# Operands of block products at alternating byte offsets, by the parity of their inner index

## Chip, cores and metric

The kernel runs on one core of one Trainium2 chip. The metric is the device time of one execution in microseconds (us). The kernel before the change takes 1253.34 us, the median of three runs (1251.72 to 1253.52).

## What is computed

A decoder trunk of two layers on 512 tokens with 1024 channels, in float32. Layer 0 mixes tokens by attention in three head groups with different dilation, layer 1 by causal pooling; a SwiGLU feed-forward network (FFN) with 2816 hidden channels follows each.

```
for i in range(DEPTH):                       # 2 layers
    if i % 2 == 0: x = x + dilated_attention_mixer(rmsnorm(x, attn_norm), w_qkv, w_attn_out)
    else:          x = x + pooling_mixer(rmsnorm(x, pool_norm), w_pool_in, w_pool_group, pool_scale)
    x = x + swiglu_ffn(rmsnorm(x, ffn_norm[i]), w_ffn_gate_up[i], w_ffn_down[i])
return rmsnorm(x, final_norm)

def swiglu_ffn(h, w_gate_up, w_down):
    gu = h @ w_gate_up
    gate, up = gu[..., :D_FF], gu[..., D_FF:]
    return (jax.nn.silu(gate) * up) @ w_down
```

## The kernel before, in words

Channels lie on the 128 partitions and tokens along them, so that a tile of 128 channels is 128x512, 2048 bytes in each partition. Every float32 matrix product is made of float32r matmuls: each operand is cut into a high part (a copy on ACT, line 96) and a low part (a subtraction on DVE, line 97), and one product of 128x128 weights with an operand takes three matmuls, high by high, high by low and low by high. Below, such three are called a **triple**. The weights are the stationary side and the operand, made from activations, is the moving side; only the attention values (lines 553 to 555) have it the other way round.

There are two kinds of products. Plain products (`Product.add`, lines 272, 273 and 275) stream 512 columns a matmul: the first q and k rows, w_out, the first five gate/up pairs of each FFN, the last part of w_down, and the pooling mixer. Block products (Strassen's seven products in place of eight) stream 256 columns: `seven` and `values12` for q, k and v, with `mult` inside (lines 391 to 393), and `chain` for the FFN's gate/up pairs and most of w_down. A product sums over an inner index k: 8 tiles in a plain product, 4 half tiles in a block product, 3 in the blocks of the FFN's second and third group. So a plain product is 24 matmuls and a block product 12 or 9, one triple for each k, all triples one behind the other on TensorE.

Operands live in **slots**, tiles of 4096 bytes in a partition: the high part in the first half, the low part in the second. Twelve slots (`FIXED`) lie in the pool `cpool`, sixteen (`SLOTS`) in the pool `fpool` that opens after the attention. `slot` takes the slot that has been free longest from one queue, and `give` puts it back. For the attention's block products some operands (`tx`) also lie in the X tiles, which are free at that time. The names of operands are h, t and tx (attention), h (plain FFN products), tb, tt and tn (gate/up pairs), hx, hy, hz and hu (w_down's blocks), a (the last hidden tiles), oh (attention's output), n and y (pooling).

Where a tile begins in its partition follows from the sizes of the tiles before it. In the built program, the X tiles and the twelve `FIXED` slots begin 128 bytes behind a multiple of 256; so do all weight tiles (whi, wlo, halfhi, halflo, in `wpool`); the sixteen slots of `fpool` begin at multiples of 256. The steps inside a tile (2048 bytes from high to low part, 1024 between halves, 512 between weight blocks) are multiples of 256. An operand and the weights are called **in phase** below when both begin alike modulo 256, and **out of phase** when they differ by 128.

The instructions of each engine run in its own order, which a scheduler fixes when the program is built, from the dependencies of the tiles: a tile that is written into a slot waits until the slot's last readers are through, and the scheduler may put it further back in an engine's order for that. Weights are loaded by SP's queue and by POOL's (the summed halves, line 158), cut by `pump` while products run, and freed when their product is through.

Of the kernel before, what the change touches and what calls it, by code (L numbers as in the profile page):

```python
# [8 lines left out]
F32 = mybir.dt.float32  # L9
F32R = mybir.dt.float32r  # L10
# [5 lines left out]
P = 128  # L16
S = 512
D = 1024
KC = D // P
# [17 lines left out]
K2 = KC // 2  # L37
# [5 lines left out]
FIXED = 12  # L43
SLOTS = 16
# [7 lines left out]
def trunk(ctx: ExitStack, tc: tile.TileContext, xT, norms, w_first, w_qk, w_qkp, w_v0, w_v0p, w_v12, w_out, w_pair, w_down, w_down0, w_down1, w_down2, w_pin, w_pgrp,  # L52
          consts, ident_in, invcnt_in, outT):
    nc = tc.nc
    cpool = ctx.enter_context(tc.tile_pool(name="cpool", bufs=1))
# [4 lines left out]
    def x_tile(k, name="x", dtype=F32):  # L60
        return cpool.tile([P, S], dtype, tag=f"x{k}", name=name)

    X = [x_tile(k) for k in range(KC)]
    nrm = cpool.tile([P, NORMS, KC], F32, name="nrm")
    ident = cpool.tile([P, P], F32, name="ident")
# [212 lines left out]
            return self  # L278


    free, pools = deque(range(FIXED)), {i: cpool for i in range(FIXED)}

    def slot(name, dtype=F32R):
        i = free.popleft()
        t = pools[i].tile([P, 2, S], dtype, tag=f"slot{i}", name=name, bufs=1)
        return i, t

    held = {}

    def give(key):  # L290
        free.append(held.pop(key))

    operand = {}

# [8 lines left out]
    def square(layer, k, engine=None):  # L303
        if layer not in acc:
            acc[layer] = tmp.tile([P, S], F32, name="acc", bufs=1)
            nc.scalar.activation(acc[layer], X[k], AF.Square)
            return
        sq = scratches[-1]("sq")
        nc.scalar.activation(sq, X[k], AF.Square)
        (engine or nc.vector).tensor_add(acc[layer], acc[layer], sq)  # L310

    def scaled(layer, k, hi, lo, on_dve=False):

        g = nrm[:, layer, k:k + 1]
        if on_dve:
            nc.vector.tensor_scalar(hi, X[k], g, None, op0=OP.mult)
        else:
            nc.scalar.activation(hi, X[k], AF.Copy, scale=g)
        nc.vector.scalar_tensor_tensor(lo, X[k], g, hi.bitcast(F32), op0=OP.mult, op1=OP.subtract)
        operand[layer, k] = hi, lo  # L320

    def note(layer, k):

        if layer < 4:
            held[layer, k], t = slot("h")
            scaled(layer, k, t[:, 0], t[:, 1])
        square(layer, k)

# [192 lines left out]
    with tc.tile_pool(name="opool", bufs=1) as opool:  # L521
        early = opool.tile([P, HEADS, S], F32R, tag="o", name="early")
        with tc.tile_pool(name="apool", bufs=1) as apool:
# [240 lines left out]
            H, T, o = {}, {}, []  # L764

            def prepare(k):

                h, t = Held("raw"), Held("raw")
                normed(0, k, rows["row"], h.t, t.t)
                for i in range(2):  # L770
                    held["h", k + i * K2], b = slot("h")
                    H[k + i * K2] = b[:, 0], b[:, 1]
                    split(*H[k + i * K2], h.t[:, i * S:(i + 1) * S])
                T["11", k] = halves_of(*H[k])[0]
                T["21", k], T["22", k] = halves_of(*H[k + K2])
                for i, names in enumerate((("1", "2"), ("3", "4"))):
                    if k < 2:
                        held["t", k, i], b = slot("t")
                        b = b[:, 0], b[:, 1]
                    else:  # L780
                        c = k - 2 + 2 * i
                        b = x_tile(c, "tx", F32R), x_tile(c + K2, "tx", F32R)
                    split(*b, t.t[:, i * S:(i + 1) * S])
                    for name, v in zip(names, halves_of(*b)):
                        T[name, k] = v
                h.done()
                t.done()
# [131 lines left out]
            for m in range(KC):  # L919
                if lead:  # L920
                    f = lead.pop(0).add([last])
                else:
                    f = Product(HEADS, heads).add(range(HEADS))
# [5 lines left out]

    with tc.tile_pool(name="fpool", bufs=1) as fpool:  # L930
        fpool.tile([P, 32], F32, name="shift", bufs=1)
        for i in range(FIXED, FIXED + SLOTS):
            free.append(i)
            pools[i] = fpool

        def unfold(m, p):

# [9 lines left out]
        def ffn(layer, nxt, lead, row, wk):  # L947
# [3 lines left out]
            pieces, T, TH, hid, act = deque(), {}, [{} for g in GROUPS], {}, []  # L951
# [3 lines left out]

            def wide(key, name):

                held[key], t = slot(name, F32)
                return t.rearrange("p a c -> p (a c)")

            def raw_hidden(j):
# [7 lines left out]
            def hide(j, gt, up):  # L969

                if j >= FC - LAST:
                    nc.vector.tensor_mul(up, up, gt)
                    held["a", j], t = slot("a")
                    act.append((t[:, 0], t[:, 1]))
                    split(*act[-1], up)
                    return
                hid[j] = raw_hidden(j)
                nc.vector.tensor_mul(hid[j], up, gt)
                g, = [g for g, (a, b) in enumerate(GROUPS) if a <= j < b]
                pieces.extend(blocks_of(g, (j - GROUPS[g][0]) // 2, hid[j - 1], hid[j]) if j % 2 else  # L980
                              half_of(g, (j - GROUPS[g][0]) // 2, hid[j]))
# [8 lines left out]
            def half_of(g, i, a):  # L990
                t = TH[g]

                def corner():
                    held["hb", g, i, 0], t["x", i] = slot("hx")
                    t["t", i] = wk.tile([P, 2 * S], F32, name="t", bufs=1)
                    t["11", i] = cut(two(t["x", i], 0), a[:, lo])

                def first():
                    v = t["t", i][:, :H2]
                    nc.vector.tensor_sub(v, a[:, hi], a[:, lo])  # L1000
                    t["1", i] = cut(two(t["x", i], 1), v)

                return corner, first

            def blocks_of(g, i, a, b):
                t = TH[g]

                def row2():
                    held["hb", g, i, 1], y = slot("hy")
                    split(y[:, 0], y[:, 1], b)  # L1010
                    t["21", i], t["22", i] = two(y, 0), two(y, 1)

                def middle():
                    v = t["t", i]
                    nc.vector.tensor_sub(v[:, H2:S], v[:, :H2], b[:, hi])
                    nc.vector.tensor_sub(v[:, S:3 * H2], b[:, hi], a[:, hi])
                    held["hb", g, i, 2], z = slot("hz")
                    split(z[:, 0], z[:, 1], v[:, H2:3 * H2])
                    t["2", i], t["3", i] = two(z, 0), two(z, 1)

                def fourth():
                    v = t["t", i]
                    nc.vector.scalar_tensor_tensor(v[:, 3 * H2:], v[:, H2:S], -1.0, b[:, lo], op0=OP.mult, op1=OP.subtract)
                    if i % 2 == 0:
                        held["hb", g, i, 3], t["u"] = slot("hu")
                    t["4", i] = cut(two(t["u"], i % 2), v[:, 3 * H2:])
                    key = ("hr", (GROUPS[g][0] + 2 * i) // 2)
                    if key in held:
                        give(key)

                return row2, middle, fourth
# [14 lines left out]
            def prepare(k):  # L1046


                h, t = wide(("hp", k), "hp"), wide(("tp", k), "tp")
                normed(op, k, row, h, t, True)  # L1050
                hq, b22 = h.rearrange("p (a b c) -> p a b c", a=2, b=2), h[:, 3 * H2:]
                held["t", k, 0], b = slot("tb")
                split(b[:, 0].rearrange("p (a c) -> p a c", a=2), b[:, 1].rearrange("p (a c) -> p a c", a=2), hq[:, :, 0])
                T["11", k], T["21", k] = two(b, 0), two(b, 1)
                for i, names in enumerate((("1", "2"), ("3", "4"))):
                    held["t", k, 1 + i], b = slot("tt")
                    split(b[:, 0], b[:, 1], t[:, i * S:(i + 1) * S])
                    for a, name in enumerate(names):
                        T[name, k] = two(b, a)
                if k % 2 == 0:  # L1060
                    held["t", k, 3], T["n"] = slot("tn")
                T["22", k] = cut(two(T["n"], k % 2), b22)
                give(("hp", k))
                give(("tp", k))
# [108 lines left out]
        with tc.tile_pool(name="pooling", bufs=6) as wk:  # L1173
# [38 lines left out]
            def mix(g):  # L1212
                for c in range(2):
                    f = Product(2, lambda k: Y[g][k], w=wg[g // 2, g % 2]).add(range(2), pos=2 * c)
                    m = 2 * g + c
                    nc.vector.scalar_tensor_tensor(X[m], f.p, nrm[:, 5, m:m + 1], X[m],
                                                   op0=OP.mult, op1=OP.add)
                    held[3, m], t = slot("n")
                    scaled(3, m, t[:, 0], t[:, 1])
                    square(3, m, nc.gpsimd)  # L1220
                for c in range(2):
                    give(("y", g, c))
# [17 lines left out]
        with tc.tile_pool(name="work1", bufs=1) as wk:  # L1240
# [46 lines left out]
            f = end(7, 1)  # L1287
# [4 lines left out]
            t = wk.tile([P, 2 * S], F32, name="t", bufs=1)  # L1292
# [87 lines left out]
```

## Time and profile before

| what | value |
|---|---|
| time, three runs | 1253.34 us median, 1251.72 to 1253.52 |
| time of the profiled execution | 1251.78 us |
| its span, first to last instruction | 1250.0 us |
| TensorE (PE) busy | 1237.6 us, 99%, 9072 matmuls |
| VectorE (DVE) busy | 1013.6 us, 81% |
| ScalarE (ACT) busy | 679.7 us, 54% |
| GpSimd (POOL) busy | 154.9 us, 12% |
| granted TensorE clock, mean | 0.996 |
| DMA | 189.91 MB, 152 GB/s over the span |

A matmul's duration in the profile is longer than its share of TensorE's time, since matmuls overlap: a 256-column matmul is shown with 0.28 us, while the next starts about 0.12 us later. What a matmul costs is therefore read from starts: a stretch of time divided by the number of matmuls that start in it. A view of a stretch counts the two or three that are still running at its begin as well.

The attention's block products lie between about 90 and 440 us, w_out up to 505, the first FFN from 509 to 840, pooling to 907, the second FFN to the end.

### The profile page before, as it was taken

What the parts mean: (1) busy time and instruction counts of PE and PEld (TensorE: products, weight loads), DVE (VectorE), ACT (ScalarE), POOL (GpSimd) and SP (SyncE); (2) the same over time, 40 slices, a digit from 0 to 9 for tenths busy, and PEclk for the clock granted to TensorE, in tenths of its full rate; (3) what the DMA queues carried; (4) which work ended last, traced back from release to release, by engine and by line L of the source; (5) the groups of instructions that cost most, each with busy time, mean ns of one, the idle gap of its engine ahead of it and who ended that gap; (6) DMA issues with size and microseconds to landing.
All of it is one profiled execution on the core that took longest, in us unless ns stands there. A gap on an engine that the chain in (4) does not pass through costs nothing. (4 is left out here: it accounts for less than half of the span.)

```text
span 1250.0 us, 23243 instructions
## 1 busy us (share of the span) xinstructions
PE 1237.6 (99%) x9072; PEld 1174.0 (94%) x9072; DVE 1013.6 (81%) x1687; ACT 679.7 (54%) x1171; POOL 154.9 (12%) x147
## 2 busy tenths in 40 slices
PE   9999999999999999999999999999999999999997
PEld 7889999999999988889999999988789999999997
DVE  7987788878778846798777878798989877888876
ACT  6444554445455544466466557563446646656652
POOL 2011111112111010101111111000310111111100
PEclk9999999999999999999999999999999999999998
DMA  8336566655756434437776786653144777677742
GB/s 291 110 85 170 134 156 145 163 131 159 182 132 161 132 138 136 113 81 194 187 186 158 177 208 163 153 181 118 51 119 117 182 182 178 153 205 190 174 116 68
DMA packets 76719, 189.91 MB, mean 152 GB/s; under 512 B 7600, under 2 KB 15936, under 8 KB 76608
## 3 DMA queue, kind: packets, MB, share of 16 engines
q1 hardware_dynamic: 51696, 142.26, 35.7%
q0 software_dynamic: 24336, 45.63, 22.5%
q8 instruction: 71, 1.16, 0.4%
q10 hardware_dynamic: 576, 0.52, 0.1%
q14 instruction: 40, 0.33, 0.1%
HBM read 186.29 MB, written 2.10 MB: 151 GB/s over the span
## 5 line engine op out<-in xcount | busy, mean ns | idle before, releaser
L96 ACT ACTIVATE whi<-raw 128x1024 fp32r<-128x1024 f32 (+2 forms) x315 | 318.7, 1016 | 248.3 <-PE seed L392 76.1
L97 DVE TENSOR_TENSOR wlo<-raw,whi 128x1024 fp32r<-128x1024 f32 (+2 forms) x315 | 367.1, 1169 | 105.3 <-ACT whi L96 104.5
L158 POOL DMA_DIRECT2D raw<-w_pair x34 | 41.1, 1209 | 310.5 <-ACT whi L96 75.4
L391 PE MATMUL sum<-tt,whi 128*128 128x256 f32 x272 | 77.0, 283 | 1.5 <-ACT seed L477 0.8
L392 PE MATMUL sum<-tt,whi 128*128 128x256 f32 x272 | 76.7, 282 | 0.0
L393 PE MATMUL sum<-tt,wlo 128*128 128x256 f32 x272 | 76.5, 281 | 0.0
L96 ACT ACTIVATE halfhi<-rawhalf 128x512 fp32r<-128x512 f32 (+1 forms) x87 | 53.2, 612 | 19.8 <-PE sum L392 12.4
L173 DVE TENSOR_TENSOR raw<-raw 128x512 f32<-128x512 f32 (+1 forms) x87 | 57.6, 662 | 2.1 <-issue 2.0
L174 DVE TENSOR_TENSOR raw<-raw 128x512 f32<-128x512 f32 (+1 forms) x87 | 57.7, 663 | 0.2
L97 DVE TENSOR_TENSOR halflo<-rawhalf,halfhi 128x512 fp32r<-128x512 f32 (+1 forms) x87 | 57.6, 664 | 0.0
L158 POOL DMA_DIRECT2D raw<-w_down x24 | 28.9, 1206 | 215.2 <-DMA raw<-w_down 34.4
L391 PEld LDWEIGHTS sum<-tt,whi 128*128 128x128 f32 x272 | 51.4, 189 | 1.9 <-ACT seed L477 1.0
L477 ACT COPY seed<-sum 128x256 f32<-128x256 f32 x58 | 20.8, 359 | 57.7 <-PE sum L393 57.5
L392 PEld LDWEIGHTS sum<-tt,whi 128*128 128x128 f32 x272 | 51.3, 189 | 0.0
L393 PEld LDWEIGHTS sum<-tt,wlo 128*128 128x128 f32 x272 | 51.2, 188 | 0.0
L391 PE MATMUL sum<-hz,whi 128*128 128x256 f32 x160 | 45.4, 284 | 0.5 <-ACT seed L477 0.3
L392 PE MATMUL sum<-hz,whi 128*128 128x256 f32 x160 | 45.3, 283 | 0.0
L392 PE MATMUL seed<-hy,whi 128*128 128x256 f32 x160 | 45.3, 283 | 0.0
L393 PE MATMUL seed<-hy,wlo 128*128 128x256 f32 x160 | 45.2, 283 | 0.0
L393 PE MATMUL sum<-hz,wlo 128*128 128x256 f32 x160 | 45.2, 283 | 0.0
L391 PE MATMUL seed<-hy,whi 128*128 128x256 f32 x160 | 45.1, 282 | 0.0
L158 POOL DMA_DIRECT2D raw<-w_qkp x18 | 22.0, 1222 | 166.4 <-DMA raw<-w_qkp 102.1
(610 smaller groups left out, 4631.7 us busy)
## 6 DMA issues: line engine op xcount, KB each, us to landing
raw<-w_pair SPq DMA_DIRECT2D x78, 512.0 KB, 4.7
raw<-w_qkp SPq DMA_DIRECT2D x36, 512.0 KB, 4.6
raw<-w_pair POOLq DMA_DIRECT2D x34, 512.0 KB, 7.6
raw<-w_down SPq DMA_DIRECT2D x32, 384.0 KB, 3.9
raw<-w_v SPq DMA_DIRECT2D x18, 512.0 KB, 4.1
raw<-w_qkp POOLq DMA_DIRECT2D x18, 512.0 KB, 7.4
rawhalf<-w_pair SPq DMA_DIRECT2D x34, 256.0 KB, 4.5
raw<-w_down SPq DMA_DIRECT2D x16, 512.0 KB, 4.9
```

Of the source, the lines that this page charges most:

```text
L96: nc.scalar.activation(hi, v, AF.Copy)
L97: nc.vector.tensor_tensor(lo, v, hi.bitcast(F32), op=OP.subtract)
L158: nc.gpsimd.dma_start(b.rearrange("p (a c) -> p a c", a=2), self.src[:, None, 3 * q:].to_broadcast([P, 2, q]), accum_op=OP.add)
L173: nc.vector.tensor_add(a[:, :q], a[:, :q], b[:, :q])
L174: nc.vector.tensor_add(a[:, q:2 * q], a[:, q:2 * q], a[:, :q])
L391: nc.tensor.matmul(dst, w.t[0][:, c], th, start=k == 0 and not onto, stop=False, skip_group_check=onto)
L392: nc.tensor.matmul(dst, w.t[0][:, c], tl, start=False, stop=False, skip_group_check=onto)
L393: nc.tensor.matmul(dst, w.t[1][:, c], th, start=False, stop=k == n - 1, skip_group_check=onto)
L477: nc.scalar.copy(e, c)
```

## The change

Slots get a side: `spread_over` makes the first half of a pool's slots, then a tile of 128 bytes (`apart`), then the second half, so that one half begins at multiples of 256 bytes and the other 128 behind. `slot` takes a slot of the side that is asked for, and one of the other side when there is none; each side has its own queue of free slots. The X tiles are laid out anew: those of odd k first, a gap of 128 bytes, those of even k. In the built program the weights still begin 128 bytes behind a multiple of 256. Side 0 is at multiples of 256 (out of phase), side 1 is in phase.

The side is the parity of the inner index k for the operands of block products; for tn and hu, where one slot holds two inner indices, it is that of k // 2. Operands of plain products ask for side 1, except oh and y, which take the default 0, as the slots for raw values do.

```
+    for k in (*range(1, KC, 2), None, *range(0, KC, 2)):
+        if k is None:
+            cpool.tile([P, 32], F32, name="gap")
+        else:
+            x_tile(k)
...
-    free, pools = deque(range(FIXED)), {i: cpool for i in range(FIXED)}
-
-    def slot(name, dtype=F32R):
-        i = free.popleft()
+    pools = {}
+    free = [[], []]
+
+    def spread_over(pool, n):
+
+        for kind in range(2):
+            for i in range(len(pools), len(pools) + n // 2):
+                pools[i] = pool
+                side[i] = kind
+                free[kind].append(i)
+                pool.tile([P, 2, S], F32R, tag=f"slot{i}", name="new", bufs=1)
+            if kind == 0:
+                pool.tile([P, 32], F32, name="apart", bufs=1)
+
+    def slot(name, dtype=F32R, kind=0):
+        i = (free[kind] or free[1 - kind]).pop(0)
         t = pools[i].tile([P, 2, S], dtype, tag=f"slot{i}", name=name, bufs=1)
         return i, t
...
-        free.append(held.pop(key))
+        i = held.pop(key)
+        free[side[i]].append(i)
+
+    side = {}
+    spread_over(cpool, FIXED)
...
-            held[layer, k], t = slot("h")
+            held[layer, k], t = slot("h", kind=1)
...
-                    held["h", k + i * K2], b = slot("h")
+                    held["h", k + i * K2], b = slot("h", kind=k % 2)
...
-        for i in range(FIXED, FIXED + SLOTS):
-            free.append(i)
-            pools[i] = fpool
+        spread_over(fpool, SLOTS)
...
-                    held["hb", g, i, 0], t["x", i] = slot("hx")
+                    held["hb", g, i, 0], t["x", i] = slot("hx", kind=i % 2)
...
-                        held["hb", g, i, 3], t["u"] = slot("hu")
+                        held["hb", g, i, 3], t["u"] = slot("hu", kind=i // 2)
```

The other `slot` calls for t, tb, tt, tn, hy, hz, a and n change in the same way. No instruction is added or removed.

By the addresses in the two built programs, a triple of a block product in `mult` follows one of the other phase 570 times of 2099 before and 1799 times with the change; in the attention's `seven` never before and 587 times of 587 with it. Of the 1320 matmuls with 512 columns, 264 are out of phase before (168 of h, 60 of n, 36 of y) and 156 with the change (96 of oh, 60 of h).

The order of instructions is the same on SP and POOL, and on all engines in the attention. It changes in the FFN, since slots are handed out in another order. On ACT, at the end of the first FFN's second group (L469 and L477, with the change L490 and L498, copy a running sum within a w_down chain; hx are the first two operands of the third group), before:

```order
L1082 COPY up<-sum 128x256
L469 COPY seed<-sum 128x256
L96 ACTIVATE hx<-hid 128x256
L96 ACTIVATE hx<-t 128x256
L477 COPY seed<-sum 128x256
L96 ACTIVATE whi<-raw 128x768 x3
```

and with the change, three chains of w_down further on:

```order
L101 ACTIVATE whi<-raw 128x768
L101 ACTIVATE whi<-raw 128x1024 x2
L101 ACTIVATE halfhi<-rawhalf 128x512
L490 COPY seed<-sum 128x256
L101 ACTIVATE hx<-hid 128x256
L101 ACTIVATE hx<-t 128x256
L498 COPY seed<-sum 128x256
```

The two hx copies move from the first to the last of the group's four w_down chains, behind the read of the slot that they now take. On DVE the two subtractions that belong to them move along; with the change they stand here, ahead of a weight tile's low part:

```order
L102 TENSOR_TENSOR halflo<-rawhalf,halfhi 128x512
L1114 TENSOR_TENSOR x<-x,seed 128x256
L102 TENSOR_TENSOR hx<-hid,hx 128x256
L102 TENSOR_TENSOR hx<-t,hx 128x256
L102 TENSOR_TENSOR wlo<-raw,whi 128x1024
```

Both move in the same way in the second FFN. Near the begin of the first FFN, among its plain gate/up pairs, ACT's copy of one hy moves from before a Silu to behind the next two copies of tt, and a later hx copy moves forward past it; before the change the piece reads:

```order
L96 ACTIVATE hx<-hr 128x256
L96 ACTIVATE hy<-hr 128x512
L1043 ACTIVATE gt<-gt 128x512
L96 ACTIVATE tb<-hp 128x512
L96 ACTIVATE tn<-hp 128x256
L96 ACTIVATE whi<-raw 128x1024
L96 ACTIVATE tt<-tp 128x512 x2
```

and with the change:

```order
L101 ACTIVATE hx<-hr 128x256
L1062 ACTIVATE gt<-gt 128x512
L101 ACTIVATE tb<-hp 128x512
L101 ACTIVATE tn<-hp 128x256
L101 ACTIVATE whi<-raw 128x1024
L101 ACTIVATE tt<-tp 128x512 x2
L101 ACTIVATE hy<-hr 128x512
```

The hy copy is now the last of these. On PE, in each FFN one triple of a gate/up pair changes places with part of the w_down product beside it.

More of the change, by code (lines that the diff above doesn't have):

```diff
@@ L777, in prepare @@
                     if k < 2:
-                        held["t", k, i], b = slot("t")
+                        held["t", k, i], b = slot("t", kind=k % 2)
                         b = b[:, 0], b[:, 1]
@@ L956, in wide @@
             def wide(key, name):
-                held[key], t = slot(name, F32)
+                held[key], t = slot(name, F32, kind=0)
                 return t.rearrange("p a c -> p (a c)")
@@ L972, in hide @@
                     nc.vector.tensor_mul(up, up, gt)
-                    held["a", j], t = slot("a")
+                    held["a", j], t = slot("a", kind=1)
                     act.append((t[:, 0], t[:, 1]))
@@ L1008, in row2 @@
                 def row2():
-                    held["hb", g, i, 1], y = slot("hy")
+                    held["hb", g, i, 1], y = slot("hy", kind=i % 2)
                     split(y[:, 0], y[:, 1], b)
@@ L1016, in middle @@
                     nc.vector.tensor_sub(v[:, S:3 * H2], b[:, hi], a[:, hi])
-                    held["hb", g, i, 2], z = slot("hz")
+                    held["hb", g, i, 2], z = slot("hz", kind=i % 2)
                     split(z[:, 0], z[:, 1], v[:, H2:3 * H2])
@@ L1051, in prepare @@
                 hq, b22 = h.rearrange("p (a b c) -> p a b c", a=2, b=2), h[:, 3 * H2:]
-                held["t", k, 0], b = slot("tb")
+                held["t", k, 0], b = slot("tb", kind=k % 2)
                 split(b[:, 0].rearrange("p (a c) -> p a c", a=2), b[:, 1].rearrange("p (a c) -> p a c", a=2), hq[:, :, 0])
@@ L1055, in prepare @@
                 for i, names in enumerate((("1", "2"), ("3", "4"))):
-                    held["t", k, 1 + i], b = slot("tt")
+                    held["t", k, 1 + i], b = slot("tt", kind=k % 2)
                     split(b[:, 0], b[:, 1], t[:, i * S:(i + 1) * S])
@@ L1060, in prepare @@
                 if k % 2 == 0:
-                    held["t", k, 3], T["n"] = slot("tn")
+                    held["t", k, 3], T["n"] = slot("tn", kind=k // 2)
                 T["22", k] = cut(two(T["n"], k % 2), b22)
@@ L1217, in mix @@
                                                    op0=OP.mult, op1=OP.add)
-                    held[3, m], t = slot("n")
+                    held[3, m], t = slot("n", kind=1)
                     scaled(3, m, t[:, 0], t[:, 1])
```

## Prediction

> **What bounds the kernel now.** First the page: TensorE is the engine that is never free. Busy time alone could hide waiting, so the waits of TensorE come next.
>
> ```profile
> span 1250.0 us, 23243 instructions
> PE 1237.6 (99%) x9072; PEld 1174.0 (94%) x9072; DVE 1013.6 (81%) x1687; ACT 679.7 (54%) x1171; POOL 154.9 (12%) x147
> ...
> PEclk9999999999999999999999999999999999999998
> ```
>
> ```profile
> PE seed L812 <- DVE idle L809: 1.2, 1, 1.2
> PE sum L391 <- ACT seed L477: 1.1, 2, 0.8
> PE ps L350 <- POOL rcol L342: 1.1, 1, 1.1
> PE sum L391 <- ACT seed L469: 0.8, 2, 0.7
> ```
>
> The four longest groups of waits come to 4.2 us of 1250, and the granted clock is full throughout. So TensorE works through one stream, and what counts is the time from one matmul's start to the next. A change of addresses acts on that, or not at all; DVE and ACT matter only where they could make the stream wait.
>
> The view by stretches shows what a matmul takes. I chose stretches that begin and end at a start of a matmul, without a wait inside, and whose phases (from the addresses) are pure.
>
> ```profile
> core 0: us, PE busy (x), PEclk, DMA share, GB/s
> 158.47:171.31 12.84, 12.84 (x110) 1.00 0.52 121
> 509.31:550.61 41.30, 41.30 (x184) 1.00 0.50 123
> 566.54:570.81 4.27, 4.27 (x38) 1.00 0.25 68
> 560.00:720.00 160.00, 160.00 (x1340) 1.00 0.73 179
> 795.03:796.70 1.67, 1.67 (x17) 1.00 0.56 99
> 802.66:804.32 1.66, 1.66 (x17) 1.00 0.62 205
> 801.02:804.20 3.18, 3.18 (x30) 1.00 0.72 209
> 856.25:861.12 4.87, 4.87 (x22) 1.00 0.62 159
> ```
>
> The count includes matmuls still running at the begin (three in the rows with x110, x17 and x30, two with x38, x184 and x1340, one with x22); by starts:
>
> - 158.47: block products of the attention, all in phase: 12.84/107 = 120.0 ns a matmul of 256 columns.
> - 566.54: gate/up products on tt and tn, all out of phase: 4.27/36 = 118.6 ns.
> - 795.03 and 802.66: w_down's blocks, the phase changing at every triple, five triples of which the first and the last are in phase: 1.67/14 = 119.3 and 1.66/14 = 118.6 ns.
> - 801.02: the same blocks where the phase goes out, in, in, out, in, in, out, in, out: 3.18/27 = 117.8 ns, the lowest over that length in the trace.
> - 509.31: plain products of the first FFN, in phase: 41.30/182 = 226.9 ns a matmul of 512 columns.
> - 856.25: plain products on h, out of phase: 4.87/21 = 231.9 ns.
> - 560 to 720, the first FFN's block part with today's mixed phases: 160.00/1338 = 119.6 ns; 17 steps in it are longer than 130 ns, by 1.2 us together, mostly at a first half weight, and without these it is 118.7 ns.
>
> So phase shows in the trace, in opposite directions: plain products want equal phase (5.0 ns of 232), block products want anything but constant equal phase (1.4 ns of 120). These rows come from different stages, which I return to among the rivals.
>
> The Trainium skill, "SBUF — State Buffer" (Who interferes with whom), gives TensorE two independent read ports, for the moving operand and for the weights, and says that it never waits on anyone; by it no byte offset would change a matmul's time and the sum below would be zero. The 231.9 beside 226.9 ns at equal shapes speak against it.
>
> **The change part by part.**
>
> 1. Attention, `seven`: 588 triples, 1764 matmuls, all in phase today at 120.0 ns (the row at 158.47). With the change all alternate. The alternating rows give 119.3 and 118.6; I take 118.9, their middle. 1764 x 1.1 = **-1.9 us**. Bounds: -3.9 us at 117.8, -1.2 at 119.3, and 0 if offsets not seen so far behave like equal phase.
>
> 2. Attention, `values12`: 224 triples, 672 matmuls, in which the operand is the stationary side and the weights stream. Today all are in phase; which side is shifted has no row. Bounds: 0, and the same 1.1 ns as in 1, 0.7 us. I take half, **-0.4 us**; a loss as large isn't excluded, since plain products show that out of phase can cost.
>
> 3. FFN, `chain`: 1512 triples, 4536 matmuls. Here the phases are mixed already and 118.7 ns is what there is to beat. Changes between triples go from 570 of 1511 to 1212. Strict alternation (118.9) gives nothing; but where one slot holds two inner indices (tn, hu) the pattern is pairs, and in the groups of three inner indices the last triple of one product and the first of the next have the same phase, as in the row at 801.02. I take 118.5, between 118.7 and the best row, nearer to the former since most products have four inner indices: 4536 x 0.2 = **-0.9 us**. Bounds: 117.8 gives -4.1 us, 119.3 gives +2.7, and 120.0 gives +5.9.
>
> 4. Plain products: 264 matmuls of 512 columns are out of phase today and 156 with the change (h and n gain, oh loses): 108 x 5.0 ns = **-0.5 us**. Both ends have rows; it is the surest term.
>
> 5. New waits. The sides halve each queue of free slots, so a slot comes round sooner. By the addresses and today's times, only three slots would be written before their last reader is through, and the scheduler has moved those writers: the hx pair at the end of the second group in both FFNs, and one hy near 535 us. For hx, ACT, DVE and PE around the new place today:
>
> ```profile
> 715.65 0.36 ACT L469 COPY seed<-sum 128x256 f32<-128x256 f32 x1
> 717.55 0.36 ACT L477 COPY seed<-sum 128x256 f32<-128x256 f32 x1 [1.53 <-PE sum L393]
> ```
>
> ```profile
> 715.45 0.27 PE L393 MATMUL ps<-hx,wlo 128*128 128x256 f32 x1
> ```
>
> ```profile
> 718.87 0.42 DVE L1095 TENSOR_TENSOR x<-x,seed 128x256 f32<-128x256 f32 x1
> 719.64 1.23 DVE L97 TENSOR_TENSOR wlo<-raw,whi 128x1024 fp32r<-128x1024 f32 x1 [0.35 <-ACT whi L96]
> ```
>
> ```profile
> 692.95 0.42 ACT L96 ACTIVATE hx<-hid 128x256 fp32r<-128x256 f32 x1 [0.22 <-DVE hid L978]
> ...
> 723.27 0.28 PE L391 MATMUL ps<-tt,whi 128*128 128x256 f32 x1
> ```
>
> The slot is last read by the triple that ends with this matmul, at 715.72. ACT, from 716.01 on, then has 1.53 us idle before its next copy, which itself waits for PE, and two hx copies take 0.42 each (row at 692.95): they fit. On DVE two subtractions of about 0.42 stand ahead of wlo; 0.35 us idle is there, so wlo is late by some 0.5 us, to 721.4. It belongs to the third product of the next pair, and at 723.27 PE only begins the second: 1.9 us of cover at least. Without that cover PE would wait 0.5 us, twice. The hx tiles themselves are read by w_down's third group, near 795 us. For hy near 535:
>
> ```profile
> 535.53 0.62 ACT L96 ACTIVATE hy<-hr 128x512 fp32r<-128x512 f32 x1
> ...
> 542.99 0.64 ACT L96 ACTIVATE tt<-tp 128x512 fp32r<-128x512 f32 x1 [1.71 <-DVE tp L508]
> 545.14 1.07 ACT L96 ACTIVATE whi<-raw 128x1024 fp32r<-128x1024 f32 x1 [1.51 <-PE ps L273]
> ```
>
> Its new place, behind the tt copy, has 1.51 us idle for its 0.62, and the Silu it leaves comes earlier. So 0, with 0.2 us as an allowance for all three: **+0.2 us**.
>
> Sum: -1.9 - 0.4 - 0.9 - 0.5 + 0.2 = **-3.5 us**. Since TensorE's stream is the span, I count it in full: a span of 1246.5 us. The profiled execution took 1251.78 us, 1.8 more than its span, so 1248.3 for such a one; it lies 1.6 us below the median of the three runs, 1253.34, and against that median the forecast is **1249.8 us**.
>
> **The rivals.**
>
> A. *Alternating is worth no more than the weaker row.* At 119.3 ns throughout, `seven` gains 1764 x 0.7 = 1.2 us, the FFN loses 4536 x 0.6 = 2.7, plain products gain 0.5 and the waits cost 0.2: +1.2 us, **1254.5 us**, slower by 0.1%, within what a measurement of this kernel can tell from no change, 0.2% or 2.5 us. For it: the FFN owes part of its 118.7 to unbroken runs out of phase (118.6 at 566.54), which the change breaks up. Against it: 117.8 at 801.02 has six changes in nine triples.
>
> B. *Offset doesn't act on the stream.* The 1.2 and 5.0 ns would then come from the stages, with their other traffic from DVE, ACT and DMA, and every term but the waits is zero: **1253.5 us**. For it: all pure in-phase block rows are from the attention. Against it: the 512-column rows at 509 and 856 are both products on h with the same weights' path. [...]
>
> C. *Slower.* The offsets matter modulo 512 and not only modulo 256. Today an operand of `fpool` lies 128 bytes ahead of the weights modulo 512. With the change, operands lie 0, 128, 256 and 384 ahead; 384 isn't in any block product today, and 256 only in the attention's tx, which are in the 120.0 row. If a change of side across those offsets loses the advantage, the FFN's products run at 120.0 and `seven` stays there: +5.9 - 0.5 + 0.2 = +5.6 us, **1258.9 us**. Place: the FFN's `chain`. It decides from a rate there above 119.3 ns (4536 x 0.6 = 2.7 us). The rows give no sign of it, beyond that they don't cover these offsets.
>
> D. *Every product as good as the best row*: 117.8 in `seven` and `chain`, 1.5 in `values12`, 0.5 in the plain ones: -3.9 - 4.1 - 1.5 - 0.5 + 0.2 = -9.8, **1243.5 us**. For it: strict alternation over more than five triples in a row has never run here.
>
> That the change doesn't do what it says is excluded for the places by the addresses: 587 of 587 changes in `seven`, 1212 of 1511 in the FFN; the missing ones are the pairs and seams of part 3 and slots taken from the other side.
>
> **How the numbers follow.** Forecast 0.55 (1247 to 1251.5 by its own bounds), A 0.17, B 0.10, C 0.10, D 0.08. The range 1245.0 to 1255.0 holds the forecast, A, B and a third of D, and leaves out C and the rest of D, some 0.16. Faster by over 0.2% (below 1250.8): 0.52 of the forecast's 0.55 and all of D, 0.60. Slower by over 0.2%: C, and 0.02 of A, 0.12. The rest, 0.28, within 0.2%.
>
> **What would show each step.** Part 1: a stretch of `seven` without a wait at 118.9 ns instead of 120.0 (12.84 us become 12.72 for the 107 matmuls); 120.0 there refutes it. Part 3: 560 to 720 us holding about 1340 matmuls instead of 1338 starts, with A at 1331. Part 4: h and n of the later plain products at 227 ns, oh of w_out up to 232. Part 5: no new line in TensorE's waits on hx, hy or whi, and the last w_down chain of the second group without a gap. The forecast is wrong above all if the alternating rows, 14 matmuls each and read to 10 ns, don't stand for long runs.

## The result, and the profile after

The changed kernel takes **1248.98 us** (median of 12 runs, 1248.01 to 1251.71) where the kernel before takes 1251.99 (12 runs beside them, 1250.91 to 1254.03): ratio 0.9976, 95% interval 0.9968 to 0.9983, so 3.0 us less. The forecast was 3.5 us less than the kernel before. The profiled execution took 1248.75 us.

The page of the changed kernel, the lines that answer to those of before:

```profile
span 1247.0 us, 23245 instructions
...
PE 1233.6 (99%) x9072; PEld 1169.0 (94%) x9072; DVE 1012.9 (81%) x1687; ACT 679.2 (54%) x1171; POOL 155.0 (12%) x147
...
PEclk9999999999999999999999999999999999999998
```

TensorE is 4.0 us less busy, DVE and ACT do the same work, and the granted clock is as it was. TensorE's longest waits in the changed kernel (line waited for, us in total, times, longest):

```profile
PE sum L412 <- ACT seed L490: 1.4, 2, 1.2
...
PE sum L412 <- ACT seed L498: 1.1, 2, 0.8
```

Of the four longest of before one has grown: L490 is the L469 of before, then 0.8 us in all with 0.7 the longest. L498 is the L477, as it was, and the other two are the same too.

The view by stretches of the changed kernel. Each row holds the same matmuls, by their place in TensorE's order, as a row of before; the first row's before, two more and the two long ones come in the fence after it, the others are in the prediction.

```profile
core 0: us, PE busy (x), PEclk, DMA share, GB/s
98.14:115.14 17.00, 17.00 (x145) 1.00 0.48 128
158.65:171.36 12.71, 12.71 (x110) 1.00 0.50 120
456.47:491.99 35.52, 35.52 (x156) 1.00 0.33 103
507.71:549.34 41.63, 41.63 (x184) 1.00 0.51 122
565.19:569.45 4.26, 4.26 (x39) 1.00 0.31 69
558.65:718.55 159.90, 159.90 (x1339) 1.00 0.72 178
718.55:739.31 20.76, 18.73 (x153) 1.00 0.84 217
794.38:796.03 1.65, 1.65 (x16) 1.00 0.39 76
800.33:803.53 3.20, 3.20 (x30) 1.00 0.79 216
855.46:860.22 4.76, 4.76 (x22) 1.00 0.62 182
```

And of the kernel before:

```profile
97.50:114.65 17.15, 17.15 (x145) 1.00 0.50 131
458.75:493.70 34.95, 34.95 (x155) 1.00 0.34 103
560.02:719.97 159.95, 159.95 (x1340) 1.00 0.73 179
719.97:740.06 20.09, 18.62 (x153) 1.00 0.85 218
```

To be read by starts (143, 107, 154, 182, 36, 1337, 150, 14, 27 and 21 matmuls): `values12` goes from 17.15/143 = 119.9 to 118.9 ns, `seven` from 120.0 to 12.71/107 = 118.8. The plain products gain on the h of the pooling mixer (4.87 to 4.76) and lose where operands now lie out of phase, w_out (34.95 to 35.52) and two of the eight h of the first FFN (41.30 to 41.63). The long FFN stretch is the same (159.95 and 159.90), and the 20 us behind it are 0.67 us longer.

Sums over all starts, from the traces of both kernels. A step from one start to the next counts as long over 130 ns, for 512 columns over 245; the mean is that of the other steps, and what the long ones take above it stands apart:

| matmuls | before: mean ns, long steps us | after | change in us |
|---|---|---|---|
| `seven`, 1764 | 119.83, 2.95 | 118.45, 3.02 | -2.4 |
| `values12`, 672 | 119.95, 0.49 | 118.96, 0.49 | -0.7 |
| `chain`, 4536 | 118.72, 6.71 | 118.48, 8.02 | +0.2 |
| plain, 1320 | 228.60, 5.22 | 228.43, 6.46 | +1.0 |
| the rest (fp32, half columns) | | | -0.9 |

That is -2.7 of the span's -3.0; the other 0.3 lies outside the first and the last start. Two of the entries are not the change's: 0.8 of the rest is one spot at the end, eight matmuls on ident that took some 210 ns each in the profiled execution before and 112 in that of every other kernel here, and some 0.9 of the plain products lies in the first 10 us, where their long steps come to 0.1 us before, 1.0 with the change, and 0.2 to 1.3 in the seven other kernels of the trunk, which do the same there.

### The profile page after: what moved, and what is told of

It is laid out like the page before. It is cut to its first block, busy times and chain, and to the rows that moved or that the text cites. A ratio compares the mean times of both kernels' runs of the same rounds, so it can differ in the third digit from the quotient of the medians.

```text
span 1247.0 us, 23245 instructions
## 1 busy us (share of the span) xinstructions
PE 1233.6 (99%) x9072; PEld 1169.0 (94%) x9072; DVE 1012.9 (81%) x1687; ACT 679.2 (54%) x1171; POOL 155.0 (12%) x147
## 5 line engine op out<-in xcount | busy, mean ns | idle before, releaser
L498 ACT COPY seed<-sum 128x256 f32<-128x256 f32 x58 | 20.8, 359 | 58.9 <-PE sum L414 58.8
```

The lines of the kernel that those rows point to most:

```text
L498: nc.scalar.copy(e, c)
```

## Experiments

**1. The streams alone.** Nothing runs but products of the kernel's two shapes, one layout after the other, 240 matmuls of 256 columns or 120 of 512 in each. The layouts, and the loop:

```python
("same", ((0, 0),)), ("off", ((128, 128),)), ("turn", ((0, 0), (128, 128))), ("pairs", ((0, 0), (0, 0), (128, 128), (128, 128))),
("far", ((256, 256),)), ("farther", ((384, 384),)), ("threeq", ((192, 192),)), ("wmove", ((128, 128, 1, 1),)),
...
h = big[:, k * STEP + a // 4:k * STEP + a // 4 + n]
l = low[:, k * STEP + b // 4:k * STEP + b // 4 + n]
for i, (w, m) in enumerate(((whi, h), (whi, l), (wlo, h))):
    nc.tensor.matmul(p[:, :n], w[:, s], m, start=k == i == 0, stop=k == K - 1 and i == 2)
```

> This kernel leaves the trunk out and copies x to the output. It runs streams of float32r matmuls alone, without other engines at work: 240 matmuls of 256 columns (120 of 512) for each way of placing operand and weights, the three matmuls of a triple as in the kernel. Theory 1 (phase modulo 256 acts on the stream by itself): same phase 120 ns, 128 bytes off 118.6, alternating by the inner index (turn) 118.5 to 119.3, pairs a little below; 256 behind like same, 384 behind like 128; with 512 columns same 227 and off 232. Theory 2 (modulo 512): 256 or 384 behind differ from same and 128 by over 0.5 ns. Theory 3 (the offset doesn't act, the differences come from the traffic of the stages): all of one width alike within 0.3 ns. Shifting the low part alone, the weights alone, or by 16 to 192 bytes has no forecast; moving operand and weights together by 128 (wmove) gives the same as same if only the difference counts.

The stretches of this run: same, off, turn, pairs, far, farther, threeq, and then same and off with 512 columns.

```profile
37.78:66.58 28.80, 28.80 (x243) 1.00 0.01 1
66.58:95.06 28.48, 28.48 (x242) 1.00 0.00 1
95.06:123.60 28.54, 28.54 (x243) 1.00 0.00 1
123.60:152.00 28.40, 28.40 (x243) 1.00 0.00 1
152.00:180.79 28.79, 28.79 (x242) 1.00 0.00 1
180.79:209.27 28.48, 28.48 (x242) 1.00 0.00 1
351.64:378.84 27.20, 27.20 (x242) 1.00 0.00 1
578.11:605.32 27.21, 27.21 (x123) 1.00 0.00 1
605.32:633.33 28.01, 28.01 (x122) 1.00 0.00 1
```

With the clock granted in full and DMA at rest: 120.0 ns in phase, 118.7 off, 118.9 in turn, 118.3 in pairs, and 226.7 against 233.4 with 512 columns. So the offset acts on the stream without any other traffic. 256 behind (28.79) is the same as in phase and 384 as 128: it counts modulo 256. Weights and operands moved together by 128 gave 120.0: by this, only their distance counts. The order in turn takes 113, 119, 120, 119, 122, 120 ns for its six matmuls, so its mean is no blend of 120.0 and 118.7 by halves. And 192 bytes gave 27.20/240 = 113.3 ns, which none of the theories had in it. With 512 columns the order in turn takes 232.1 ns, where halves of 226.7 and 233.4 would give 230.1: an operand in phase gains little beside one that is not.

**2. Every distance in steps of 16 bytes.** The same kernel with other layouts:

```diff
-    ("same", ((0, 0),)),
...
+    *((f"b{c}", ((16 * i, 16 * i),)) for i, c in enumerate(LETTERS)),
+    ("hlow", ((192, 0),)),
+    ("hhigh", ((0, 192),)),
+    ("hturn", ((192, 192), (0, 0))),
```

> This kernel leaves the trunk out and copies x to the output. Streams of float32r matmuls as in the first such kernel, with operand and weights apart by every multiple of 16 bytes from 0 to 240 (names b and a letter for 256 columns, p and a letter for 512, a for 0, i for 128, m for 192), and with only the high part, only the low part or every second triple at 192. Theory 1 (the phase modulo 256 sets a matmul's time): 0, 64, 128 and 192 come out as measured before, 120.0, 117.8, 118.7 and 113.3 ns; the others lie on a curve between, with its lowest point at 192 or beside it. A rival (192 was low by something else, its place in the stream): 192 is not below 117 ns again.

Measured, ns a matmul by how far the operand lies behind the weights, modulo 256:

| bytes | 0 | 16 | 32 | 48 | 64 | 80 | 96 | 112 | 128 | 144 | 160 | 176 | 192 | 208 | 224 | 240 |
|---|---|---|---|---|---|---|---|---|---|---|---|---|---|---|---|---|
| 256 columns | 120.0 | 118.7 | 116.7 | 118.3 | 117.8 | 120.0 | 120.0 | 113.3 | 118.7 | 118.7 | 117.3 | 119.3 | 113.3 | 119.2 | 118.3 | 117.1 |
| 512 columns | 226.7 | 231.7 | 233.3 | 233.3 | 228.9 | 231.1 | 233.4 | 231.1 | 232.4 | 233.3 | 234.3 | 233.3 | 233.3 | 234.6 | 233.3 | 226.7 |

The rows for 112 and 192 bytes with 256 columns, and for 192 and 240 with 512:

```profile
237.25:264.45 27.20, 27.20 (x242) 1.00 0.01 1
378.19:405.39 27.20, 27.20 (x242) 1.00 0.01 1
...
965.29:993.29 28.00, 28.00 (x122) 1.00 0.00 1
1049.43:1076.63 27.20, 27.20 (x121) 1.00 0.00 1
```

There is no smooth curve, against theory 1. The low point at 192 came again (113.3 in both kernels), so its place in the stream isn't the reason; 112 was measured here alone. With 512 columns, 128 gave 233.4 ns in experiment 1 and 232.4 here, so differences of 1 ns there mean little. The change's pair of distances, 0 and 128, is the slowest value and a middling one; 192 in turn with 0 gave 116.7.

**3. The attention's part alone.** The change's layout; the attention asks for sides, and everything behind it takes the slot that has been free longest, so that the order of instructions is that of before:

```diff
-    def slot(name, dtype=F32R, kind=0):
+    def slot(name, dtype=F32R, kind=None):
+        if kind is None:
+            kind = min((k for k in range(2) if free[k]), key=lambda k: since.get(free[k][0], 0))
...
-                    held["hb", g, i, 0], t["x", i] = slot("hx", kind=i % 2)
+                    held["hb", g, i, 0], t["x", i] = slot("hx")
```

> Layout of the change; the attention's operands ask for their side, everything behind the attention takes the slot that has been free longest of both sides, as before. Theory 1: seven and values12 gain as in the change (2.4 and 0.7 us in its trace), chain keeps 118.7 ns, plain products lose 1.0 us (474 matmuls out of phase against 264 before): 2 us faster than before, 0.2%. If the gain came from the FFN's order of slots: no faster than before.

1251.34 us (11 runs) against 1252.82; ratio 0.9993, interval 0.9984 to 1.0002: 0.9 us by the ratio where 2 were expected, and not clear of no change. Its stretches on the same `seven` and on the first FFN's h:

```profile
158.23:170.94 12.71, 12.71 (x109) 1.00 0.53 121
507.41:549.67 42.26, 42.26 (x183) 1.00 0.50 120
```

`seven` and `values12` gain as in the whole change (118.45 and 118.96 ns, 3.0 us together). 2.2 us go back in the plain products, where 1.0 was expected. 474 of their matmuls, not 264, are out of phase here, but that is only a part. By the sides of its slots the h of this stretch is in phase and out of phase in turn, nearly throughout, and the whole runs at 42.26/182 = 232.2 ns, as the order in turn does alone. Over all plain products, those in phase take 229.6 ns where they took 227.7 before, and those out of phase 231.7. The `chain` runs at 118.62, and its long steps come to 7.42 us.

**4. The FFN's part alone.** The attention's slots all in phase; the FFN asks for sides, with 14 slots in each:

```diff
-        spread_over(fpool, SLOTS)
+        fpool.tile([P, 32], F32, name="shift", bufs=1)
+        spread_over(fpool, SLOTS, SLOTS - 2)
```

> The attention as before, all in phase; the FFN asks for sides as in the change (14 slots out of phase, 14 in phase). Theory 1: seven 119.8 ns as before; chain 118.5 instead of 118.7, 1.0 us; 24 instead of 264 plain matmuls out of phase, 1.1 us; together 2 us faster than before if no new waits come, 0.5 to 1 us faster if chain waits longer as in the change. Theory 3: no difference.

1250.56 us against 1252.82; 0.9985, interval 0.9977 to 0.9994. The `chain` has 118.47 ns as in the change, a rate worth 1.1 us, but its long steps take 8.3 us where they took 6.7; plain products, with 24 out of phase, take 1.0 us less. `seven` stays at 119.83. So the FFN's part is clear of no change, at 1.9 us by the ratio. With experiment 3 the ratios add up to that of the change: 0.07% and 0.15% are 2.8 of the 3.0 us, though the first could be zero by its interval.

**5. Everything in phase.** The kernel before without the shift of the FFN's slots:

```diff
-        fpool.tile([P, 32], F32, name="shift", bufs=1)
```

> The kernel before without the 128 bytes ahead of the FFN's pool: every operand in phase. Theory 1: chain goes from 118.7 to 119.8 or 120 ns, 5.4 us slower, plain products gain 1.2 us: 4 us slower than before, 0.3%. Theory 3: no difference.

1255.16 us against 1252.82; 1.0018, interval 1.0010 to 1.0027: 2.3 us slower, in the expected direction, where 4 were expected. The long FFN stretch and the one on tt and tn:

```profile
567.81:572.13 4.32, 4.32 (x38) 1.00 0.24 68
561.21:722.33 161.12, 161.12 (x1339) 1.00 0.72 178
```

4.32/36 = 120.0 ns, and the `chain` has 119.92 throughout: 5.4 us more than 118.72, with 1.5 us back in the plain products and 1.2 in shorter waits. So the mixture in the kernel before, which came of that shift and of the order in which slots came free, already held most of what offsets of 128 can give the FFN.

**6. All operands 192 bytes behind the weights.** Experiment 5's kernel, its weights and buffers moved:

```diff
-    tmp.tile([P, 64], F32, name="shift", bufs=1)
+    wpool.tile([P, 16], F32, name="shift", bufs=1)
+    tmp.tile([P, 112], F32, name="shift", bufs=1)
```

> The kernel before, with everything in phase by the FFN pool's 128 bytes taken out, and then the weights moved 64 bytes on, so that operands lie 192 bytes behind the weights modulo 256 (values12, where the sides are swapped, 64). Nothing else is changed. Theory 1: the stream sets the time, so chain gains 4536 x 5.4 ns = 24.5 us, seven 1764 x 6.5 = 11.5, values12 672 x 2.2 = 1.5; plain products between 227 and 232 ns, +0 to +5 us: 32 to 37 us faster than before, 2.6 to 3%. Rival (DVE, busy for 81% of the span and cutting the weights, becomes the bound): a part of it comes back as waits of TensorE on wlo, 15 to 25 us faster remain.

1238.58 us against 1252.35; 0.9898, interval 0.9883 to 0.9912: 12.8 us faster, less than either theory said (32 to 37, or 15 to 25), and a third of the 40 us that 113.3 ns would be worth in all block products (1764 x 6.5, 4536 x 5.4 and 672 x 6.6 ns). A plain stretch, and two of `chain`, in successive chains of w_down with the same operands at the same distance:

```profile
505.66:548.13 42.47, 42.47 (x184) 1.00 0.49 120
608.02:614.71 6.69, 6.69 (x62) 1.00 0.78 195
616.46:623.53 7.07, 7.07 (x63) 1.00 0.91 222
```

Plain products run at 42.47/182 = 233.4 ns and lose 6.9 us. The `chain` runs at 6.69/59 = 113.4 ns up to a wait, and at 7.07/60 = 117.8 after it, for whole products. There are two levels: of the stretches of twelve `chain` matmuls without a long step, 228 run at 113 or 114 ns, 52 at 118 and 2 at 116. Over all it is 114.28 in `chain`, 116.12 in `seven`, 117.77 in `values12` (where the distance is the other way round, 64, alone 117.8). And the long steps of `chain` grew from 6.7 to 15.2 us. So the rates of the block products gave 28 us; 8.7 went back in their long steps and 6.9 in the plain products. The waits that the rival named, on wlo, come to 0.2 us.

**7. The hx pair put back.** The change, but the third group's two hx take the other side, where slots are long free; on ACT and DVE they stand where they stood before the change:

```diff
-                    held["hb", g, i, 0], t["x", i] = slot("hx", kind=i % 2)
+                    held["hb", g, i, 0], t["x", i] = slot("hx", kind=((1 - i % 2) if g == 2 else i % 2))
```

> The change, but with the two hx tiles of the third group of each FFN on the other side, so that they get slots that are long free and stand in ScalarE's and VectorE's order where they stood before the change. The alternation in the FFN stays (1225 of 1511 triples change phase, 1211 in the change); 24 more plain matmuls are out of phase, which costs 0.1 us. Theory: the longer waits near 733 us (2.6 us above the rate in the change and in the FFN part alone, 2.0 to 2.2 in the kernels that keep the order) come from the moved hx pair, so they return to 2.0 to 2.2 here and the time is 0.3 to 1 us less than the change's 1249.0. Rival: the waits come from TensorE's being earlier there against the loads; then they stay at 2.6 and the time is the change's within 0.2 us or so.

First what happens there. In the changed kernel DVE makes the pair's two subtractions ahead of wlo (rows of before in the prediction):

```profile
717.86 0.42 DVE L102 TENSOR_TENSOR hx<-hid,hx 128x256 fp32r<-128x256 f32 x1
718.20 0.42 DVE L102 TENSOR_TENSOR hx<-t,hx 128x256 fp32r<-128x256 f32 x1
718.53 1.22 DVE L102 TENSOR_TENSOR wlo<-raw,whi 128x1024 fp32r<-128x1024 f32 x1
```

TensorE is 1.42 us earlier here than before (the stretches begin at 718.55 and 719.97), wlo only 1.11 us. So wlo is 0.31 us late. But it isn't behind the wait that has grown, which is this one:

```profile
734.82 0.39 PE L412 MATMUL sum<-tt,whi 128*128 128x256 f32 x1 [1.21 <-ACT seed L490]
```

The copy on L490 stands in ACT's order behind a copy of weights, here before the change and with it:

```profile
733.08 1.06 ACT L96 ACTIVATE whi<-raw 128x1024 fp32r<-128x1024 f32 x1 [2.95 <-DMA raw<-w_pair]
```

```profile
732.34 1.06 ACT L101 ACTIVATE whi<-raw 128x1024 fp32r<-128x1024 f32 x1 [3.49 <-PE sum L414]
```

In both traces this copy starts 0.16 us after a load of POOL's queue has landed (at 732.92 and 732.18), also where the row names TensorE. POOL's load adds to what a load of SP's queue has brought, and its row begins 1.2 us after that one has landed (at 723.11 and 722.24). The two loads, before and then with the change:

```profile
717.16 0.33 SPq L155 DMA_DIRECT2D raw<-w_pair  x1
724.34 1.20 POOL L158 DMA_DIRECT2D raw<-w_pair  x1 [7.94 <-ACT seed L469]
```

```profile
715.82 0.33 SPq L160 DMA_DIRECT2D raw<-w_pair  x1
723.46 1.21 POOL L163 DMA_DIRECT2D raw<-w_pair  x1 [8.00 <-ACT seed L490]
```

Counted from the begin of the stretch, SP's load is issued at the same place (2.81 us ahead before, 2.73 with the change), and POOL's is 0.54 us late (4.37 and 4.91 us behind it). SP's load is issued 2.7 us before the late wlo begins, so wlo can't be what delays it. In experiment 7, the stretch, POOL's load and ACT's copy:

```profile
718.51:738.73 20.22, 18.65 (x153) 1.00 0.82 216
```

```profile
722.89 1.20 POOL L163 DMA_DIRECT2D raw<-w_pair  x1 [8.06 <-ACT seed L490]
```

```profile
731.75 1.06 ACT L101 ACTIVATE whi<-raw 128x1024 fp32r<-128x1024 f32 x1 [3.06 <-DMA raw<-w_pair]
```

POOL's load is at 4.38 us again, and the stretch takes 20.22 us, against 20.76 in the change and 20.09 before. The rival, that TensorE is earlier there, falls with the same stretch in experiments 3 and 4:

```profile
718.88:739.02 20.14, 18.59 (x152) 1.00 0.82 216
719.95:740.52 20.57, 18.62 (x153) 1.00 0.86 217
```

In experiment 3 TensorE is 1.09 us earlier than before and the pair stands where it stood; in experiment 4 TensorE is where it was and the pair has moved. With experiment 5's 20.15, the four traces with the pair at its old place have 20.09 to 20.22 us and the two with it moved 20.57 and 20.76. So the moved pair (and the triple on TensorE that changes places with it) costs some 0.5 us there. How, isn't shown: a load that SP issues between 11.6 and 11.8 us ahead of the stretch in all six lands 5.3 to 5.5 us ahead of it in the four and 4.9 in the two, which is before ACT comes to the pair's new place (at 714.62, 3.9 us ahead).

The time is 1249.46 us against 1252.34, ratio 0.9977, interval 0.9966 to 0.9987: no faster than the change, against the expectation. In its trace the long steps of `chain` come to 7.95 us, nearly those of the change; the half microsecond has come back in other waits, among them two of 0.2 us near 1121 and 1212 us.

**8. Blocks at 192, plain products in phase, halves of a weight in one buffer.** On experiment 6; plain weights start 48 columns, 192 bytes, further into their buffer:

```diff
-            if ring in ("w", "half"):
+            if ring == "w":
+                t = wpool.tile([P, 2 * n + 64], F32R, tag=ring, name=ring, bufs=BUFS[ring])
+                self.t = [t[:, 48 * plain + i * n:48 * plain + (i + 1) * n] for i in range(2)]
+            elif ring == "half":
```

> All operands lie 192 bytes behind a multiple of 256 from the weights of the block products, as in the run with 192 bytes, but the weights of the plain products lie 192 bytes further back in their buffer, so that the plain products are in phase again. If the plain products' 6.9 us of loss in that run come from their distance alone, they go back to about 227.7 ns a matmul and the time to 1231 to 1233 us (median of the other run 1238.6, ratio to the kernel before about 0.984). If instead the plain products lost because everything around them ran faster, they stay near 233 ns and the time near 1238. That the high and low halves of a weight now share one buffer may make a load start a little later: up to 1 us.

1241.44 us against 1252.34; 0.9906, interval 0.9892 to 0.9920, where 1231 to 1233 were expected. The plain products are at 227.4 ns, so their 6.9 us did come from the distance alone. But the block products' long steps take 27.2 us, where in experiment 6 they took 18.9 by the same measure (the next expectation puts these at 27.6 and 15.5), and the whole is no faster.

**9. The same with buffers of their own.** Again on experiment 6, and the buffers' 256 bytes more each are taken from the memory for descriptors:

```diff
+            if ring == "w":
+                self.t = [wpool.tile([P, n + 64], F32R, tag=ring + c, name=ring + c, bufs=BUFS[ring])[:, 48 * plain:48 * plain + n] for c in ("hi", "lo")]
...
-    nc = bacc.Bacc("TRN2", target_bir_lowering=False, num_devices=1, dynamic_dma_scratch_size=8192)
+    nc = bacc.Bacc("TRN2", target_bir_lowering=False, num_devices=1, dynamic_dma_scratch_size=6144)
```

> As the run that put the plain products back in phase, but with the high and low halves of a weight in buffers of their own again; the 256 bytes a buffer that this needs come from the memory kept for GpSimd's DMA descriptors, which shrinks from 8192 to 6144 bytes. Theory: in the run before, the shared buffer brought the longer waits (long steps 27.6 us above the rate in the block products, 15.5 in the run with 192 bytes and buffers of their own); without it they fall back to about 15 us, the plain products stay at 227.4 ns, and the time is 1231 to 1234 us, ratio to the kernel before about 0.984. Rival: the waits come from the products' being faster than weights are brought and split; then the time stays near 1240, as in both runs before.

**1232.16 us** against 1253.36; ratio 0.9833, interval 0.9820 to 0.9847, 21 us faster than the kernel before and by the ratios 18 faster than the change. The products on tt and tn in experiment 8 and in this one:

```profile
560.77:565.57 4.80, 4.39 (x38) 1.00 0.32 95
```

```profile
559.95:564.03 4.08, 4.08 (x39) 1.00 0.31 87
```

The same 36 matmuls take 4.80 us with 0.41 idle in them, and 4.08 without a gap. The block products' long steps are 16.9 us here, the plain products 227.3 ns. The smaller memory for descriptors is the only other difference between the two kernels, so it was the shared buffer that made them wait. By the rates, the block products gain 24.8 us and the plain ones 1.7; 6.7 us go back in the block products' long steps.

## Why the prediction was right

1. **`seven`**: right, a little short. Forecast -1.9 at 118.9 ns; measured -2.4, 118.45 in the mean and 118.8 in the stretch that was named. Taking the middle of two rows of 14 matmuls held up: alone, the order in turn takes 118.9.
2. **`values12`**: forecast half the rate, -0.4; it took all of it, 119.95 to 118.96, -0.7. So it gains with the operand as the stationary side too, if less than `seven` (1.0 ns against 1.4).
3. **`chain`**: the rate was right, 118.48 against 118.5, -1.1 us against -0.9. That pairs help is borne out alone (118.3 in pairs, 118.9 in turn). How much of the FFN's rate they give was not tried by itself.
4. **Plain products**: called the surest term, and overrated, -0.2 by the rate instead of -0.5. Out of phase they take 231.9 ns and in phase 228.0 after the change, 3.9 apart where one pair of rows had said 5.0, and the in-phase ones rose by 0.3. The price per matmul was taken as fixed, but it depends on the neighbours too (experiments 1 and 3).
5. **New waits**: the step that failed. It allowed 0.2 us; the long steps of `chain` grew by 1.3. What it checked came out: wlo is late, by 0.31 us, and no wait on it came. But it looked for the price only at the instructions' new places. Near 733 us the moved pair costs some 0.5 us by way of loads that are late before its new place is reached (experiment 7); how the one leads to the other stays open. And waits grew without any moved writer: in experiment 3, whose order is that of before on every engine, the long steps of `chain` come to 7.42 us, 0.7 more than before, and with the hx pair back in its place they stay at 7.95. The sum had no term for waits that come with a faster stream or another layout. The waits on whi, a sign named for this step, have a new line of 0.3 us (L843), but it lies in the first 12 us, where no order has changed.

With these put right the sum reads -3.5 - 0.5 - 0.3 - 0.2 + 0.3 + 1.1 = -3.1 us, beside -3.0 by the medians: the forecast came out because gains that were put too low met waits that were put too low. That these two cancelled is luck; that the stream gains by the order in turn is not.

**The rivals.** A needed 119.3 ns; `seven` and the stream alone say 118.5 to 118.9. B fell with experiment 1: 120.0 and 118.7 with no other engine at work. The Trainium skill, "SBUF — State Buffer" (Who interferes with whom), has TensorE's two reads on independent ports; by that rule the two stretches of 28.80 and 28.48 us would be one, and the measurement decides. C fell with experiment 1 too, 256 being the same as 0 and 384 as 128. D, which took 117.8 for the best a product can have, was wrong for alternation and far too modest for other distances.

## What to carry to other kernels

Where TensorE is busy 99% and each matmul brings its own weights, time the stream by itself over the distance between operand and weights modulo 256 bytes, for every width of product, before choosing a layout; here one distance was worth 5.6% of a product of 256 columns and cost 3% of one of 512, so each shape had to get its own. When a wait has grown, follow it back from the matmul that waits, through the copy to the loads, with times counted from one and the same matmul in both kernels, before blaming the instruction that was moved: here the load was late before that instruction ran. Don't count on the rate of the stream alone, nor on all of its gain: of those 40 us, 21 arrived with everything in place. In that trace the block products' rates gave 25 and the plain products 2, and waits took 7.

## What the runs showed of the hardware

- The time of an fp32r matmul that loads its own weights depends on the distance of operand and weights in SBUF modulo 256 bytes: 113.3 to 120.0 ns with 256 columns, 226.7 to 234.6 with 512, with nothing else running. The best distances differ: 112 and 192 for the one, 0 and 240 for the other.
- With the high part of the operand in phase and the low part 128 off, the stream alone took 117.8 ns; the other way round 119.9. With 512 columns, triples in phase and out of phase in turn took 232.1 ns, not the 230.1 between 226.7 and 233.4. So a matmul's time depends on its neighbours' distances too.
- At one distance there is more than one steady rate. In experiment 6 `chain` ran at 113.4 ns before a wait and at 117.8 after it; the stretch of `seven` at 158 us ran at 113.6 (12.15 us) in that trace and at 117.8 (12.60) in experiment 9's, with the same distances (rows below, of experiment 6 and of experiment 9). What sets which rate follows a wait, these runs don't show.

```profile
159.53:171.68 12.15, 12.15 (x109) 1.00 0.53 127
```

```profile
158.18:170.78 12.60, 12.60 (x109) 1.00 0.50 123
```
